# Second groups' B and C tiles moved ahead of x tiles 6 to 9, one more gate tile among the scan's chunks, two PSUM edits in the turn

## The chip, the cores and the metric

One core of a Trainium2 chip runs the whole program. The metric is the device time of one execution in microseconds (us), the median of several runs. The engines named here are PE (TensorE, matmuls), DVE (VectorE), ACT (ScalarE), POOL (GpSimd) and SP (SyncE, which only issues transfers here). Each works through its own queue in order.

## The reference

One layer of a hybrid decoder step over 1024 prompt positions and 8 sample positions (1032 columns), width 1024. Cut to what matters:

```
hn = rmsnorm(x, norm1_w);  proj = hn @ w_in
z, xbc, dt_raw, v = split(proj, [1536, 1536 + 2048, 1536 + 2048 + 24])
xbc = silu(causal_dwconv(xbc, conv_buf, conv_w, conv_b))        # width 4
xs, bm, cm = split(xbc)                                         # 24 heads x 64 | 4 groups x 64 | 4 groups x 64
dt = softplus(dt_raw + dt_bias);  a = -exp(a_log)
# chunked scan, chunks of 128 positions
cb = einsum('bclgn,bcsgn->bclsg', cc, bc)
mix = cb * decay * dt;  y_diag = einsum('bclsgr,bcsgrp->bclgrp', mix, xc)
chunk_states = einsum(bc, decay_to_end * dt, xc);  h = chunk_decay * h + chunk_states
y_off = einsum(cc, h_in, exp(acum))
y = (y_diag + y_off + d_skip * xs) * silu(z);  y = grouped rmsnorm(y)
x = x + concat([y, pool_mixer(v)]) @ w_out
u = causal_dwconv(rmsnorm(x) @ w_up);  x = x + (silu(gate) * val) @ w_down
```

The states after the step are outputs too.

## The kernel before

Everything is held transposed: a tile has 128 channels on the partitions and the 1032 positions along the free axis. The input projection has 32 such tiles, each eight k-tiles deep: x tiles 0 to 11, B tiles 12 and 13, C tiles 14 and 15 (the conv tiles, which get conv and SiLU), z tiles 16 to 27 (the gate tiles) and four pooling tiles. Tiles 12 and 14 are B and C of the first two state groups (q = 0, heads of x tiles 0 to 5), tiles 13 and 15 those of the second two (q = 1, x tiles 6 to 11).

A float32 weight is split into a high and a low part (ACT copies the high part, `lo_eng`, DVE or POOL, subtracts the low one), so a product costs three matmuls. `gemm` takes a tile in three chunks of 344 columns: 24 matmuls into one of the PSUM banks of tag g (three in this part of the program), then ACT copies the result out. In front of each chunk `gemm` runs the work due from `later` and then calls `between`, if there is one.

A conv tile (`conv_tile`) loads its weights by two transfers on SP, sets the borders of its buffer u with two small POOL operations, copies the three chunks into u on ACT (L464 to L467), copies the new conv state on POOL, then multiplies by the first tap on ACT (L477), adds three taps on DVE (L479), and in front of the next chunk asks ACT for the SiLU. A gate tile (`gate_tile`) copies z out on ACT (L652), and in front of a later chunk takes its SiLU and multiplies it into the x tile on DVE (L657, L659); after each third tile the group norm follows (squares on ACT, sums on POOL, L679 on PE, L688 on DVE).

The scan runs over eight chunks of 128 positions for each q. One step of it is made of three parts:

- `decay(q, c)`: a broadcast transfer into `mix`, a clamp on DVE (L501), twelve exponentials on ACT, and for c > 0 the same for `ce`, with a product on POOL (L516).
- `turn(q, c)`: PE transposes B of the chunk (L528) into a bank of tag pM, of which there is one, and ACT copies it to bT. PE forms C·B (L534) and transposes three x tiles (L537) into each of two banks of tag pT; DVE copies the x part to `xd` (L538), masks the C·B part (L539), scales xd (L541) and multiplies the mask product into `mix` (L546).
- `apply(q, c)`: PE forms the chunk's state into pM (L560) and its output into two banks of tag pY (L583, L593); POOL decays the old state (L569), DVE adds the new one (L573, which frees pM), and DVE adds the output to the x tiles (L601).

`ssd_tasks(q)` puts ten tasks into a queue: the first decay, and steps c = -1 to 7, each of which applies chunk c, turns chunk c + 1 and starts the decay of chunk c + 2. `between` adds a rate to a credit in front of every projection chunk and takes one task for each full credit. The rate is 0.6, starting from 0.35, for the scan's tasks: three tasks in five chunks. The sample positions have a task for each x tile (`sample_tile`): a state load, five POOL operations, a store, a reduction on DVE (L638) and an update of the x tile (L639), all with single buffers.

The order in `ssd_phase` before is: conv tiles 1 to 5; tiles 6 to 11 with the scan's tasks of q = 0; tiles 13 and 15 with six samples at rate 1.0; gate tiles 0 to 5 with the scan's tasks of q = 1, which bring the other six samples along. Behind that, in `project`, with other PSUM pools, come gate tiles 6 to 11, the pooling groups, the output projection and then the FFN. The order of the source is not the order of execution: when the program is built, each engine's list is ordered by a simulated timeline (`schedule_with_timeline_sim=True`), with the dependencies and the number of buffers kept.

Of the kernel before, what the change touches and what calls it, by code (L numbers as in the profile page):

```python
# [12 lines left out]
AF = mybir.ActivationFunctionType  # L13
# [59 lines left out]
class Kernel:  # L73
# [445 lines left out]
    def turn(self, q, c, mix):  # L519

        nc = self.nc
        cols = slice(c * P, (c + 1) * P)
        b, cc = self.bt[q], self.ctl[q]
        xd = self.ph.tile([P, 2, 12, 64], F32, tag="xd", name=self.nm("xd"), bufs=1)
        cb = self.ph.tile([P, 2, P], F32, tag="cb", name=self.nm("cb"), bufs=1)
        bT = self.ph.tile([P, P], F32, tag="bT", name=self.nm("bT"), bufs=1)
        pc = self.bank("pM")
        nc.tensor.transpose(pc[:, 0:P], b[:, cols], self.ident)  # L528
        nc.scalar.activation(bT, pc[:, 0:P], AF.Copy)

        pts = [self.bank("pT") for _ in range(2)]
        for g, pt in enumerate(pts):
            rows = slice(64 * g, 64 * g + 64)
            nc.tensor.matmul(pt[:, 384:512], b[rows, cols], cc[rows, cols], start=True, stop=True)  # L534
        for g, pt in enumerate(pts):
            for i in range(3):
                nc.tensor.transpose(pt[:, i * P : (i + 1) * P], self.xs[6 * q + 3 * g + i][:, cols], self.ident)  # L537
            nc.vector.tensor_copy(xd[:, 0, 6 * g : 6 * g + 6].rearrange("p r x -> p (r x)"), pt[:, :384])  # L538
            nc.vector.tensor_tensor(out=cb[:, g], in0=pt[:, 384:512], in1=self.mat[:, M_TRI : M_TRI + P], op=ALU.mult)  # L539
        hs = slice(c * NH + 12 * q, c * NH + 12 * q + 12)  # L540
        nc.vector.tensor_tensor(  # L541
            out=xd[:, 1], in0=xd[:, 0], in1=self.wd[:, hs].unsqueeze(2).broadcast_to([P, 12, 64]), op=ALU.mult
        )
        for g in range(2):
            part = mix[:, 6 * g : 6 * g + 6]
            nc.vector.tensor_tensor(  # L546
                out=part, in0=part, in1=cb[:, g].unsqueeze(1).broadcast_to([P, 6, P]), op=ALU.mult
            )
        return xd, bT
# [142 lines left out]
    def project(self):  # L692

        nc, d, tc = self.nc, self.d, self.tc
        self.bcd = self.dram.tile([2, NB, 2 * P], F32, name="bcd")
        self.xs, self.bt, self.ctl = [None] * XT, {}, {}

        with ExitStack() as outer:
            with self.banks(g=3, pT=2, pY=2, pM=1) as self.ps:
                self.startup([(n, n) for n in (12, 14, 0)])  # L700
                self.pu = outer.enter_context(tc.tile_pool(name="u", bufs=1))
                with tc.tile_pool(name="ssd", bufs=1) as self.ph:
                    self.ssd_phase()
            with self.banks(g=4, pT=2, pY=1, pM=1) as self.ps, tc.tile_pool(name="mix", bufs=1) as self.ph:
                for i in range(6, 12):
                    self.gate_tile(16 + i, i, None)
                self.pool_groups()

    def ssd_phase(self):
        nc, d = self.nc, self.d  # L710
        self.hst = {}
        queue = []

        credit = [0.0, 0.0]

        def between():
            credit[0] += credit[1]
            while credit[0] >= 1.0 and queue:
                credit[0] -= 1.0
                queue.pop(0)()  # L720
            if not queue:
                credit[0] = 0.0

        def flush():
            while queue:
                queue.pop(0)()

        def ssd_tasks(q):
            dec, trn = {}, {}

            def start():
                dec[0] = self.decay(q, 0)

            def step(c):
                if c >= 0:
                    self.apply(q, c, *dec.pop(c), *trn.pop(c))
                if c + 1 < NCH:
                    trn[c + 1] = self.turn(q, c + 1, dec[c + 1][0])
                if c + 2 < NCH:
                    dec[c + 2] = self.decay(q, c + 2)  # L740
                if c == -1:
                    self.sample_bc(q)
                if q == 1 and 1 <= c < 7:
                    sample(5 + c)

            queue.append(start)
            for c in range(-1, NCH):
                queue.append(lambda c=c: step(c))

        def sample(i):  # L750
            with self.behind(self.pl):
                self.sample_tile(i // 6, i)

        self.lo_eng = nc.gpsimd
        for n in range(1, 6):
            self.keep(n, self.conv_tile(n, n, None))
        ssd_tasks(0)
        credit[:] = 0.35, 0.6
        for n in range(6, 12):
            self.keep(n, self.conv_tile(n, n, between))  # L760
        flush()
        self.lo_eng = nc.vector
        for i in range(6):
            queue.append(lambda i=i: sample(i))
        credit[1] = 1.0
        for n in (13, 15):
            self.keep(n, self.conv_tile(n, n, between))
        flush()
        nc.sync.dma_start(d["conv_o"], self.conv_st)
        ssd_tasks(1)  # L770
        credit[:] = 0.35, 0.6
        for i in range(6):
            self.gate_tile(16 + i, i, between)
        flush()
        self.run_due()
# [697 lines left out]
```

## Time and profile before

| | us |
|---|---|
| median of 3 runs | 1450.8 (1449.79 to 1450.92) |
| the profiled execution | 1453.59 |
| its span in the profile | 1451.8 |
| PE busy in the span | 1376.6 (95%) |
| DVE busy | 976.9 (67%) |
| ACT busy | 701.4 (48%) |
| POOL busy | 517.4 (36%) |

The span is what the profiler's records cover; the difference to the execution's time lies around it. A busy time is a sum over stages with different limits, so it is read stage by stage. Rows of a timeline give the start, the duration, engine, line, operation, output and inputs, and in brackets the idle time of that engine just before and what ended it. "Granted clock" is the share of TensorE's full clock; it is 1.00 or 0.50 at any moment here, and a mean between in a longer stretch.

### The profile page before, as it was taken

How to read it: one execution, taken by the hardware profiler on the slowest of the kernel's cores; microseconds unless marked ns; L12 is line 12 of the kernel's file. 1: busy time of each engine (PE TensorE's matmuls, PEld its weight loads, DVE VectorE, ACT ScalarE, POOL GpSimd, SP SyncE). 2: the span in 40 equal slices, each digit the busy share in tenths (PEclk: the TensorE clock that was granted, in tenths of full speed). 3: DMA queues.
4: the chain of work that ended last, by engine and by line, in shares of the span. 5: the costliest groups of instructions: out<-in, count | busy, mean ns of one | idle time of the engine just before them, and what ended most of it. 6: DMA issues, size and time to landing. Idle time of an engine off the chain costs nothing.

```text
span 1451.8 us, 26584 instructions
## 1 busy us (share of the span) xinstructions
PE 1376.6 (95%) x10312; PEld 1325.7 (91%) x10312; DVE 976.9 (67%) x1474; ACT 701.4 (48%) x1396; POOL 517.4 (36%) x581
## 2 busy tenths in 40 slices
PE   8999999788899999999969999999999998999997
PEld 6899879768699999999959999999999998999997
DVE  6475998587853484744786777777777775567743
ACT  6247763465455451312454455554555554444441
POOL 5242566567421105765342222212222213113121
PEclk9999999999899999999989999999999999999999
DMA  6031334244311146676467778777777769457513
GB/s 241 8 105 52 117 128 149 91 139 120 109 39 39 45 144 234 229 239 195 141 152 159 204 190 201 187 204 185 189 177 194 201 217 346 135 187 234 176 51 118
DMA packets 126683, 227.56 MB, mean 157 GB/s; under 512 B 27852, under 2 KB 45084, under 8 KB 126556
## 3 DMA queue, kind: packets, MB, share of 16 engines
q1 hardware_dynamic: 88620, 143.62, 31.9%
q0 software_dynamic: 24208, 61.30, 17.2%
q10 hardware_dynamic: 13728, 20.93, 4.5%
q8 instruction: 81, 1.33, 0.4%
q14 instruction: 46, 0.38, 0.1%
HBM read 169.11 MB, written 45.15 MB: 148 GB/s over the span
## 4 chain that ended last, share of the span: by engine, by line
PE 81%; DVE 10%; DMA 3%; issue 3%; ACT 1%; POOL 1%; SPq 0%; DVEq 0%; ACTq 0%; POOLq 0%
PE g L1025 30%; PE g L1172 16%; PE g L157 10%; PE g L156 10%; PE g L158 10%; DMA mix<-acd 1%; DVE mix L546 1%; DVE mix L501 1%; PE pY L583 1%; DVE xs L601 1%; DVE xs L479 1%; DVE x L932 1%; DVE op L208 1%; DVE wop L138 1%; DVE xd L541 1%
## 5 line engine op out<-in xcount | busy, mean ns | idle before, releaser
L1025 PE MATMUL g<-op,wop 128*128 128x258 f32 x3696 | 451.3, 285 | 15.8 <-ACT wop L137 5.8
L1025 PEld LDWEIGHTS g<-op,wop 128*128 128x128 f32 x3696 | 449.8, 191 | 17.1 <-ACT wop L137 6.0
L1172 PE MATMUL g<-op,wop 128*128 128x258 f32 x1848 | 231.1, 288 | 9.2 <-ACT op L207 5.6
L1172 PEld LDWEIGHTS g<-op,wop 128*128 128x128 f32 x1848 | 228.0, 193 | 11.2 <-ACT op L207 6.0
L137 ACT ACTIVATE wop<-raw 128x512 fp32r<-128x512 f32 (+1 forms) x208 | 125.8, 607 | 229.8 <-PE g L158 126.7
L156 PE MATMUL g<-hh,wop 128*128 128x344 f32 x696 | 227.3, 327 | 4.2 <-ACT u L464 3.5
L158 PE MATMUL g<-hh,wop 128*128 128x344 f32 x696 | 226.6, 326 | 0.0
L157 PE MATMUL g<-hl,wop 128*128 128x344 f32 x696 | 225.8, 324 | 0.0
L138 DVE TENSOR_TENSOR wop<-raw,wop 128x512 fp32r<-128x512 f32 (+1 forms) x186 | 139.4, 756 | 119.0 <-ACT wop L137 113.4
L137 ACT ACTIVATE wop<-s 128x512 fp32r<-128x512 f32 (+1 forms) x136 | 83.5, 619 | 134.7 <-PE g L1172 47.3
L1004 POOL DMA_DIRECT2D s<-s x44 | 38.3, 870 | 284.9 <-DMA s<-wup 123.8
L156 PEld LDWEIGHTS g<-hh,wop 128*128 128x128 f32 x696 | 132.9, 191 | 7.2 <-ACT u L464 4.1
L158 PEld LDWEIGHTS g<-hh,wop 128*128 128x128 f32 x696 | 132.7, 191 | 1.3 <-issue 1.1
L157 PEld LDWEIGHTS g<-hl,wop 128*128 128x128 f32 x696 | 133.0, 191 | 0.6 <-issue 0.5
L1072 DVE SCALAR_TENSOR_TENSOR acc<-u,cst,acc 128x1048 f32<-128x1048 f32 x88 | 115.1, 1308 | 11.6 <-ACT acc L1070 10.1
L138 DVE TENSOR_TENSOR wop<-s,wop 128x512 fp32r<-128x512 f32 (+1 forms) x136 | 91.2, 677 | 34.8 <-ACT wop L137 32.4
L1060 DVE TENSOR_TENSOR u<-u,g 128x258 f32<-128x258 f32 (+2 forms) x176 | 58.6, 356 | 83.3 <-PE g L1025 81.0
L1057 ACT ACTIVATE u<-g 128x258 f32<-128x258 f32 (+2 forms) x220 | 69.5, 340 | 81.9 <-PE g L1025 76.3
L157 PE MATMUL g<-yl,wop 128*128 128x344 f32 x288 | 92.6, 323 | 3.0 <-DVE yl L208 3.0
L1142 POOL DMA_DIRECT2D g<-td x77 | 41.9, 548 | 143.9 <-DVE op L208 69.0
L158 PE MATMUL g<-yh,wop 128*128 128x344 f32 x288 | 92.4, 322 | 0.0
L156 PE MATMUL g<-yh,wop 128*128 128x344 f32 x288 | 91.9, 322 | 0.0
(265 smaller groups left out, 2294.6 us busy)
## 6 DMA issues: line engine op xcount, KB each, us to landing
s<-wup SPq DMA_DIRECT2D x88, 256.0 KB, 3.2
g<-td POOLq DMA_DIRECT2D x77, 258.0 KB, 4.5
raw<-wup SPq DMA_DIRECT2D x66, 256.0 KB, 4.4
raw<-win SPq DMA_DIRECT2D x58, 256.0 KB, 2.6
mix<-acd SPq DMA_DIRECT2D x16, 768.0 KB, 6.0
td<-acc ACTq DMA_DIRECT2D x22, 516.0 KB, 5.7
s<-wup POOLq DMA_DIRECT2D x44, 256.0 KB, 5.5
s<-s POOLq DMA_DIRECT2D x44, 256.0 KB, 3.9
```

What stands on the lines that cost most here:

```text
L137: self.nc.scalar.activation(hi, raw[:, :w], AF.Copy)
L138: lo_eng.tensor_tensor(out=lo, in0=raw[:, :w], in1=hi.bitcast(F32), op=ALU.subtract)
L156: nc.tensor.matmul(ps[:, :n], wh, xh[:, sl], start=(first and k == 0), stop=False)
L157: nc.tensor.matmul(ps[:, :n], wh, xl[:, sl], start=False, stop=False)
L158: nc.tensor.matmul(ps[:, :n], wl, xh[:, sl], start=False, stop=(final and k == last))
L1004: nc.gpsimd.dma_start(t, raw[acc] if acc in raw else w[acc][j], accum_op=ALU.add)
L1025: nc.tensor.matmul(out, a, b, start=(p in OPENS and j == 1), stop=(j == 12), skip_group_check=True)
L1057: a = nc.scalar.activation(out, ps[:, s], AF.Copy, scale=-1.0 if p in ("p5", "p4") else 1.0)
L1060: nc.vector.tensor_tensor(out=out, in0=out, in1=ps[:, s], op=op)
L1072: nc.vector.scalar_tensor_tensor(out=acc, in0=u[:, k : k + FW], scalar=self.c("fw", 3 * n + k), in1=acc, op0=ALU.mult, op1=ALU.add)
L1142: self.loaded = self.nc.gpsimd.dma_start(st[:, j], self.td[i + j][ROW[p]]).ins
L1172: self.pe = nc.tensor.matmul(out, a, b, start=(s == 0 and i == 0 and j == 0), stop=(s == len(PIECES) - 1 and i == nk - 1 and j == 2),).ins
```

## The change

The transposed B goes into a bank of tag g; the copy of the transposed x goes from DVE to ACT; conv tiles 13 and 15 come ahead of tiles 6 to 9 among the first groups' tasks; tiles 10 and 11 come with the samples, at rate 0.7 and without emptying the queue behind them; gate tile 0 follows at that rate, ahead of the second groups' tasks' own rate, which now runs over gate tiles 1 to 6; gate tile 6 leaves the part behind.

```diff
@@ turn
-        pc = self.bank("pM")
+        pc = self.gps()
         nc.tensor.transpose(pc[:, 0:P], b[:, cols], self.ident)
...
-            nc.vector.tensor_copy(xd[:, 0, 6 * g : 6 * g + 6].rearrange("p r x -> p (r x)"), pt[:, :384])
+            nc.scalar.activation(xd[:, 0, 6 * g : 6 * g + 6].rearrange("p r x -> p (r x)"), pt[:, :384], AF.Copy)
@@ project
-                for i in range(6, 12):
+                for i in range(7, 12):
                     self.gate_tile(16 + i, i, None)
@@ ssd_phase
         ssd_tasks(0)
         credit[:] = 0.35, 0.6
-        for n in range(6, 12):
+        for n in (13, 15, 6, 7, 8, 9):
             self.keep(n, self.conv_tile(n, n, between))
         flush()
         self.lo_eng = nc.vector
         for i in range(6):
             queue.append(lambda i=i: sample(i))
-        credit[1] = 1.0
-        for n in (13, 15):
+        credit[1] = 0.7
+        for n in (10, 11):
             self.keep(n, self.conv_tile(n, n, between))
-        flush()
         nc.sync.dma_start(d["conv_o"], self.conv_st)
+
         ssd_tasks(1)
+        self.gate_tile(16, 0, between)
         credit[:] = 0.35, 0.6
-        for i in range(6):
+        for i in range(1, 7):
             self.gate_tile(16 + i, i, between)
         flush()
         self.run_due()
```

## The prediction

> **What bounds the kernel now.** I read the slices of the page first, then the busy time by stage, then PE's waits, then the timelines of PE, ACT and DVE at the place of the longest wait. The PE row of the page says that TensorE is the engine to look at, and that the eighth to the eleventh of its 40 slices (36.3 us each), in the chunked scan, hold the longest run in which it isn't full:
>
> ```profile
> PE   8999999788899999999969999999999998999997
> ```
>
> The view by stretches (columns: stretch, length, then busy us of PE, PEld, DVE, ACT, POOL with their instruction counts, the granted clock, DMA share, GB/s):
>
> ```profile
> 139.00:240.00 101.00, 95.50 (x838) 83.67 (x837) 93.60 (x135) 68.98 (x156) 60.72 (x47) 1.00 0.40 127
> 240.00:283.50 43.50, 34.29 (x216) 33.42 (x215) 26.48 (x26) 11.81 (x21) 26.66 (x26) 0.99 0.38 118
> 283.50:411.00 127.50, 114.46 (x847) 96.75 (x848) 106.80 (x157) 74.19 (x164) 76.68 (x47) 0.90 0.35 107
> 280.00:290.00 10.00, 6.55 (x28) 6.33 (x29) 6.42 (x10) 7.65 (x21) 0.00 (x0) 0.66 0.17 55
> ...
> 411.00:483.00 72.00, 72.00 (x446) 70.08 (x445) 24.02 (x36) 37.04 (x54) 10.03 (x6) 1.00 0.13 41
> ```
>
> Call the first three stages A (x tiles with the first groups' chunks), B (B and C tiles with the samples) and C (gate tiles with the second groups' chunks). PE idles 101.00 - 95.50 = 5.5 us in A, 9.2 in B and 13.0 in C. In C the granted clock is 0.90, so another 127.5 x 0.10 = 12.8 us go to half-speed stretches. Together 40.5 us, the most that the change can win. The last row is the stretch behind them, gate tiles alone: PE 72.00 of 72.00 at clock 1.00. So what PE gains ahead of 411 us is kept there; and 18 projection chunks in 72 us make 4.0 us a chunk. In C DVE is busy 106.80 of 127.50 (84%), in A 93.60 of 101.00 (93%): the scan is near DVE's limit, and PE's gaps are its echo.
>
> PE's waits in 60 to 430 us (waiter, whom it waits for, total us, times, longest):
>
> ```profile
> PE pM L528 <- DVE h L573: 9.4, 6, 3.4
> PE pT L534 <- ACT xs L185: 5.7, 1, 5.7
> PE pY L583 <- DVE mix L546: 4.2, 3, 2.2
> PE g L156 <- ACT u L464: 3.5, 2, 2.5
> ```
>
> Three of these four are what the edits aim at: the transposed B waiting for bank pM, the second groups' first chunk waiting for a SiLU, and the mask product.
>
> **Part 1, the order of the tiles.** The 5.7 us are one wait. PE's row, then ACT's and DVE's around it:
>
> ```profile
> 283.45 0.80 PE L534 MATMUL pT<-xs,xs 64*128 64x128 f32 x4 [5.71 <-ACT xs L185]
> ```
>
> ```profile
> 271.89 0.46 ACT L652 ACTIVATE z<-g 128x344 f32<-128x344 f32 x1
> 282.32 1.08 ACT L185 ACTIVATE xs<-xs 128x1056 f32<-128x1056 f32 x1 [9.96 <-DVE xs L479]
> ...
> 288.24 0.43 ACT L652 ACTIVATE z<-g 128x344 f32<-128x344 f32 x1
> ```
>
> ```profile
> 273.43 1.30 DVE L479 SCALAR_TENSOR_TENSOR xs<-u,cst,xs 128x1056 f32<-128x1056 f32 x1
> 279.01 0.69 DVE L638 TENSOR_REDUCE dx<-stt 128x8 f32<-128x512 f32 x1 [4.27 <-POOL stt L637]
> 279.61 1.31 DVE L479 SCALAR_TENSOR_TENSOR xs<-u,cst,xs 128x1056 f32<-128x1056 f32 x1
> ```
>
> The SiLU of the last C tile sat 9.96 us at the head of ACT's queue, because DVE's three conv taps (L479) were cut in two by a sample's reduction (L638) that waited 4.27 us for POOL. PE stood from 277.74 to 283.45, and the clock of 280 to 290 us was 0.66: 3.4 us more. Gross 9.1 us.
>
> By the credits, before, the second groups' first turn is asked for ahead of the third chunk of gate tile 0: two chunks (8 us) behind the last conv tile. After, B and C are ready since the first two tiles, the last conv tile is x tile 11, and three chunks of gate tile 0 and two of gate tile 1 (20 us) come first. The 12 us more exceed the 5.7. The samples spread too: at 0.7 a chunk, four fall into x tiles 10 and 11 and two into gate tile 0, against three in each of tiles 13 and 15. What is late next: PE may run two chunks on, but the z of gate tile 0's second chunk was copied only at 288.24, behind the SiLU in ACT's queue. If that SiLU is as late as now, the copy ends near 283.45 + 0.4 and PE, out of its three g banks one chunk past 277.7 (281.7), waits about 2 us. If the fifth and sixth sample stand behind the taps it waits nothing. I take the middle, 1.1: **-8.0 us** (bounds -9.1 and 0).
>
> The moved tiles issue what they issued: each two weight loads on SP, two small POOL fills of u, one conv_st copy. The low weight parts of tiles 13 and 15 go from DVE to POOL, and those of 10 and 11 from POOL to DVE: no change in sum. The conv_o store still waits on SP for the last conv tile's copy on POOL, with the gate weights behind it, as now. The two L464 waits (3.5 us) in B come from the same queue of SiLU and samples; I leave them (bounds -3.5 and, with six samples at the same POOL pace, +3.5). Gate tile 6 moved ahead of the boundary costs PE the same three chunks; it fills scan gaps rather than a stretch that is 72.00 of 72.00 busy. Without gaps to fill it is worth nothing.
>
> **Part 2, copies from DVE to ACT.** Groups of the view by form (busy us, mean ns, idle before): DVE in C (283 to 411 us), then ACT in C, then DVE in A (108 to 241 us).
>
> ```profile
> L546 DVE TENSOR_TENSOR mix<-mix,cb 128x768 f32<-128x768 f32 x16 | 23.1, 1442 | 0.1
> ...
> L538 DVE COPY xd<-pT 128x384 f32<-128x384 f32 x16 | 8.8, 547 | 3.6 <-PE pT L537 2.8 <-PE pY L583 0.7
> L539 DVE TENSOR_TENSOR cb<-pT,mat 128x128 f32<-128x128 f32 x16 | 4.4, 278 | 0.0
> ```
>
> ```profile
> L185 ACT ACTIVATE mix<-mix,acl 128x128 f32<-128x128 f32 x96 | 28.9, 388 | 19.0 <-DVE mix L501 19.0
> ...
> L566 ACT ACTIVATE h<-pM 128x384 f32<-128x384 f32 x1 | 0.5, 493 | 0.0
> ```
>
> ```profile
> L546 DVE TENSOR_TENSOR mix<-mix,cb 128x768 f32<-128x768 f32 x16 | 17.3, 1082 | 0.8 <-ACT mix L185 0.8
> ```
>
> Sixteen copies of 547 ns leave DVE in C: 8.8 us, and A issues the same sixteen. ACT takes each at the 493 ns of L566, the same shape out of a bank: 7.9 us a stage, on top of 68.98 in 101.00 and 74.19 in 127.50, so ACT comes to 76% in A and 64% in C. In C DVE is the limit for 84% of the time: 0.84 x 8.8 = 7.4, less a little for the copies' hand-over, **-7 us** (bounds 0 and -8.8). Not more, because the product L546 is 1442 ns here against 1082 in A with POOL beside it, and that doesn't go. In A the loss is only 5.5; I take **-4** together with part 3 (bounds 0 and -5.5).
>
> **Part 3, the bank of the transposed B.** Two rows of the view by stretches, of the places behind the two longest of its waits:
>
> ```profile
> 320.00:330.00 10.00, 6.62 (x57) 5.88 (x56) 10.00 (x12) 6.17 (x17) 7.56 (x6) 0.84 0.49 172
> 340.00:350.00 10.00, 9.56 (x53) 9.11 (x54) 7.35 (x17) 7.50 (x16) 3.14 (x3) 0.83 0.92 232
> ```
>
> The 9.4 us of L528 go, since a g bank was emptied two chunks earlier. In A (2.4 of them) that is gain. In C (7.0) the h add that PE waited for was late because DVE's line was full; PE now passes it, runs on into projection matmuls, and meets L583 waiting for L546 of the same line. So I count nothing beyond part 2 (bounds 0 and -7.0, and -3.3 of clock, 10 us at 0.84 and 10 at 0.83).
>
> The price: three g banks now carry sixteen more tenants. A bT copy stuck behind a SiLU in ACT's queue would hold one; cover is the chunk that PE has in the other banks, 4.0 us; without it each 2 us more of SiLU wait are 2 us of PE.
>
> **Sum:** -8 - 4 - 7 = -19 us against the profiled execution, 1453.59 us (span 1451.8 and 1.8 around it): 1434.6. The median shown is 2.8 below that execution, so about 1432.
>
> **Rivals.** (1) *The stall moves.* The order on each engine comes from a timeline simulated at build, not from the source: the first turn stood in the source ahead of gate tile 0's third chunk and ran inside gate tile 1's first. If it is again put where SiLU 11 is late, part 1 gives nothing: -11, 1440. Against it: the source distance grows by 12 us.
> (2) *Two readers of one bank.* The copy on ACT and the cb product on DVE (L539) read one pT bank. If one has to wait for the other, two products of 278 ns and their hand-over lie in the chain of each of 16 steps: 16 x 0.56 = 9 us given back: -10, 1441. No row shows ACT and DVE in one pT bank. The Trainium skill, PSUM — Partial Sum Buffer, section PSUM bank collisions raise a hardware error, says that two engines may not be in one bank and quadrant at once, two reads included; by that rule the build must order them, and no run here shows it yet.
> (3) *ACT's queue, slower than before.* ACT waits 19.0 us in C at the heads of the exponentials for L501, 2.4 a step. A copy queued behind that wait holds xd, thus L541, L560 and the bank. With that wait before the copy in every step of both stages (16 x 2.4 = 38 us), a third covered by PE's chunks, 25 us come on and only part 1's 8 and part 2's 11 go off: +6, 1457. It decides from 1.2 us of uncovered delay a step (19/16). For it: ACT runs in order and DVE's copy never stood behind exponentials. Against it: the copies of a turn come ahead of the next-but-one chunk's exponentials in the source.
> (4) *More.* With DVE relieved the gaps in C fall under what costs the clock, and half of C's 25.8 us goes: -5 - 9 - 13 = -27, 1424.
>
> **Chances.** Forecast 0.45, (1) 0.18, (2) 0.10, (3) 0.14, (4) 0.13. A measurement of this kernel can tell about 0.2% (2.9 us) from no change. Faster: 0.45 + 0.13 and 0.22 of the 0.28 of (1) and (2), 0.80; the other 0.06 within; slower 0.14. The range, 1418 to 1452, leaves out (3) and what may lie beyond (4).
>
> **What would show it.** Right: no wait of L528; no L534 wait on the SiLU and a clock of 1.00 at the end of B; sixteen L538 copies of about 0.49 us on ACT in each stage and DVE's busy time in C near 98; PE's waits in C on L546 shorter in sum than 11 us. Wrong: waits of PE on z or u copies (L652, L464) of over 4 us, L541 waiting on ACT's L538, or half clock at the boundary of B and C as now.

## The result, and the profile after

The changed kernel takes **1460.9 us** (median of 5 runs, 1457.3 to 1462.5) against 1450.8 before: ratio 1.0066, 95% interval 1.0045 to 1.0087. It is slower by about 10 us, where 1432 was forecast, and lies 9 us above the range. The profiled execution of after took 1460.94 us (span 1459.2), 7.4 us more than that of before.

The same view by stretches as in the prediction, of the kernel after (length, busy us of PE, PEld, DVE, ACT, POOL, granted clock, DMA share, GB/s). The last row takes the scan as a whole:

```profile
139.00:240.00 101.00, 95.02 (x754) 80.50 (x753) 75.76 (x108) 73.22 (x167) 49.35 (x41) 0.93 0.33 104
240.00:283.50 43.50, 41.09 (x291) 39.96 (x290) 33.45 (x36) 13.24 (x24) 32.79 (x30) 1.00 0.47 145
283.50:411.00 127.50, 109.37 (x785) 91.29 (x784) 95.60 (x131) 80.33 (x179) 71.70 (x50) 0.89 0.35 111
...
127.00:430.00 303.00, 276.48 (x2050) 240.83 (x2050) 219.29 (x296) 184.31 (x399) 158.92 (x125) 0.93 0.34 106
```

And the last row's like of before:

```profile
127.00:430.00 303.00, 275.26 (x2089) 243.79 (x2088) 239.83 (x334) 174.46 (x370) 168.99 (x127) 0.95 0.35 109
```

DVE was relieved of 20 us, just as the change says, and PE's busy time is no lower. What grew is the time at half clock: before lost 27.7 us of idle PE and 303 x 0.05 = 15.2 of clock, together 43; after lost 26.5 and 303 x 0.07 = 21.2, together 48. (The clock is given to two places, so each sum is good to some 1.5 us.) Over the whole spans the granted clock is 0.968 against 0.973, or 46.7 against 39.2 us, and these 7.5 us are about what the two executions differ by. PE's waits of after, 60 to 440 us, show that the idle time has other causes than before:

```profile
PE pT L534 <- DVE cb L539: 16.6, 5, 6.3
PE g L156 <- ACT z L652: 5.2, 2, 2.6
PE g L156 <- ACT u L464: 2.4, 2, 1.6
PE pY L583 <- DVE mix L546: 1.3, 1, 1.3
```

The waits of L528 (9.4) and of L534 on the SiLU (5.7) are gone, and those of L583 on L546 fell from 4.2 to 1.3. In their place L534 waits 16.6 us, in five places, for the mask product that empties its pT bank. Three of the five, from PE's timelines:

```profile
159.54 0.44 PE L537 MATMUL pT<-mat,xs 128*128 128x128 f32 x2
161.23 0.27 PE L528 MATMUL g<-mat,xs 128*128 128x128 f32 x1
161.43 1.53 PE L583 MATMUL pY<-mix,xd 128*64 128x128 f32 x24
...
171.24 0.79 PE L534 MATMUL pT<-xs,xs 64*128 64x128 f32 x2 [3.48 <-DVE cb L539]
...
220.50 0.48 PE L534 MATMUL pT<-xs,xs 64*128 64x128 f32 x2 [2.50 <-DVE cb L539]
...
400.15 0.79 PE L534 MATMUL pT<-xs,xs 64*128 64x128 f32 x2 [6.29 <-DVE cb L539]
```

The rows of after by stretches that hold the first two:

```profile
220.00:230.00 10.00, 9.51 (x49) 7.11 (x51) 4.49 (x8) 7.74 (x19) 1.83 (x1) 0.66 0.00 0
170.00:180.00 10.00, 8.76 (x48) 7.78 (x50) 4.40 (x7) 9.32 (x22) 3.25 (x2) 0.66 0.00 0
```

Each of them has a clock of 0.66: 6.8 us at half speed, up to 3.4 us of work lost at gaps of 3.48 and 2.50 us. Stage A, where before had a clock of 1.00, now has 0.93. DVE isn't full: it is busy for 4.4 of these 10 us, and for 75.76 of 101.00 in stage A, against 93.60 before. ACT's timeline ahead of the first gap, and DVE's at it:

```profile
162.32 1.08 ACT L185 ACTIVATE xs<-xs 128x1056 f32<-128x1056 f32 x1 [2.39 <-DVE xs L479]
163.41 1.28 ACT L178 ACT_TABLE_LOAD   x1
164.70 3.62 ACT L185 ACTIVATE mix<-mix,acl 128x128 f32<-128x128 f32 x12
168.23 0.83 ACT L185 ACTIVATE ce<-ce 128x768 f32<-128x768 f32 x1
169.08 1.28 ACT L178 ACT_TABLE_LOAD   x1
170.37 0.87 ACT L538 ACTIVATE xd<-pT 128x384 f32<-128x384 f32 x2
```

```profile
170.90 0.29 DVE L539 TENSOR_TENSOR cb<-pT,mat 128x128 f32<-128x128 f32 x1 [0.66 <-ACT xd L538]
```

Read it backwards. PE had the transposes of this turn done at 159.98. Their copy could not have run before 162.96 on any engine, since `xd` has one buffer, which the matmuls of the chunk before (L583) read until then. It stood in ACT's queue behind a SiLU that waited for the conv taps, a table load, twelve exponentials, `ce` and another table load, and ran at 170.37, 7.4 us later. The mask product on DVE followed it, and only then was the bank free for the C·B of the next turn. The bracket names DVE's L539, because it came last; the delay is ACT's.

The second gap is of another kind. ACT's row and DVE's rows ahead of it, and then those ahead of the wait of 2.47 us that ends at 369.59:

```profile
217.38 0.87 ACT L538 ACTIVATE xd<-pT 128x384 f32<-128x384 f32 x2
...
217.87 2.37 DVE L501 SCALAR_TENSOR_TENSOR mix<-acl,mix 128x1536 f32<-128x1536 f32 x1
220.16 0.47 DVE L539 TENSOR_TENSOR cb<-pT,mat 128x128 f32<-128x128 f32 x2
```

```profile
364.29 0.87 ACT L538 ACTIVATE xd<-pT 128x384 f32<-128x384 f32 x2
...
368.11 1.23 DVE L659 TENSOR_TENSOR xs<-xs,z 128x8 f32<-128x8 f32 x1
369.26 0.28 DVE L539 TENSOR_TENSOR cb<-pT,mat 128x128 f32<-128x128 f32 x1
```

Here ACT's copies were over 1.9 and 4.1 us before the product began, and DVE had other work in front of it: a clamp of the next decay, or the group norm, the output adds and the gate products. The wait of 1.91 us that ends at 336.06 is like them, with 5.0 us between copy and product. So 6.9 of the 16.6 us are made by the product's place in DVE's line. Before, DVE took a turn's first product right behind its copy; with the copy on ACT, other work stands between. At 400 us ACT is late again, with a z SiLU in place of the conv tile's, and the product then waits another 0.8 us for the gate product on DVE.

### The profile page after: what moved, and what is told of

Its sections match the earlier page's. It is cut to its first block, busy times and chain, and to the rows that moved or that the text cites. A ratio compares the mean times of both kernels' runs of the same rounds, so it can differ in the third digit from the quotient of the medians.

```text
span 1459.2 us, 26569 instructions
## 1 busy us (share of the span) xinstructions
PE 1383.0 (95%) x10312; PEld 1328.2 (91%) x10312; DVE 958.0 (66%) x1442; ACT 713.1 (49%) x1428; POOL 496.9 (34%) x581
## 4 chain that ended last, share of the span: by engine, by line
PE 80%; DVE 7%; ACT 4%; DMA 3%; POOL 2%; issue 2%; SPq 0%; DVEq 0%; ACTq 0%; POOLq 0%
PE g L1026 30%; PE g L1173 15%; PE g L156 10%; PE g L157 10%; PE g L158 10%; ACT mix L185 1%; PE pY L583 1%; DMA st<-st_ssm 1%; DVE mix L546 1%; PE pY L593 1%; POOL st L635 1%; DVE mix L501 1%; DVE op L208 1%; DVE x L933 1%; ACT L178 1%
## 5 line engine op out<-in xcount | busy, mean ns | idle before, releaser
L1173 PEld LDWEIGHTS g<-op,wop 128*128 128x128 f32 x1848 | 227.6, 193 | 12.4 <-ACT op L207 6.1
L138 DVE TENSOR_TENSOR wop<-raw,wop 128x512 fp32r<-128x512 f32 (+1 forms) x186 | 133.9, 726 | 116.8 <-ACT wop L137 116.0
```

What stands on the lines that cost most here:

```text
L138: lo_eng.tensor_tensor(out=lo, in0=raw[:, :w], in1=hi.bitcast(F32), op=ALU.subtract)
L1173: self.pe = nc.tensor.matmul(out, a, b, start=(s == 0 and i == 0 and j == 0), stop=(s == len(PIECES) - 1 and i == nk - 1 and j == 2),).ins
```

## The experiments

The three edits are called R (the order of the tiles), P (the transposed B in a g bank, L528) and X (the xd copies L538 on ACT); after is R, P and X together. Ratios are against before, with runs of before on the same chip beside them. The letters in the expectations name theories, which the text behind them takes up.

### One edit at a time

Each kernel is before with one part of the diff above, or (e_rp) after with X undone:

```diff
@@ e_rp, turn
-            nc.scalar.activation(xd[:, 0, 6 * g : 6 * g + 6].rearrange("p r x -> p (r x)"), pt[:, :384], AF.Copy)
+            nc.vector.tensor_copy(xd[:, 0, 6 * g : 6 * g + 6].rearrange("p r x -> p (r x)"), pt[:, :384])
```

> The change with the copy of the transposed x back on DVE (L538 as before), all else as changed. Theory Q (the copies in ACT's queue hold the pT banks, because the mask product L539 waits for the copy and the next C.B matmul waits for both): the 16.6 us of L534 waits and the half-speed stretches behind them go, 1435 to 1445 us, faster than before. Theory O (the new order of tiles is what costs): it stays at 1455 or above. Theory G (the transposed B takes a g bank from the projection): it stays at 1455 or above, with waits of the projection on L652 or L464.

> The kernel before with the copy of the transposed x on ACT and nothing else. Theory Q: slower than before by 5 to 20 us, with new waits of PE at L534 for the mask product L539. Theories O and G: faster than before by 3 to 10 us, since 17.6 us leave DVE and neither the order nor the bank is changed.

> The new order of tiles alone: transposed B in pM and the copies on DVE as before. Theory Q: faster than before by 5 to 10 us, the 5.7 us wait of L534 on the SiLU gone and the L528 waits still there. Theory O: slower than before by 5 us or more.

> The transposed B in a g bank alone, order and copies as before. Theory Q: no L528 wait; DVE's line stays as full, so 0 to 6 us faster. Theory G: slower than before by 3 us or more, with more waits of the projection on the copies out of g banks.

| | ratio | 95% interval | median us |
|---|---|---|---|
| e_r | 0.9982 | 0.9966 to 0.9998 | 1447.3 |
| e_x | 0.9959 | 0.9942 to 0.9977 | 1443.0 |
| e_p | 0.9995 | 0.9981 to 1.0009 | 1448.2 |
| e_rp | 0.9988 | 0.9973 to 1.0004 | 1447.7 |

No edit is slower by itself. R is worth 2.6 us, X 5.9, and P nothing that can be measured; their sum is -9.3 us, and together they cost +9.6. Every theory that puts the loss down to one edit is out: Q, which had e_x slower by 5 to 20 us and e_rp at 1435 to 1445, O, which had e_r slower, and G, which had e_p slower. The 19 us come from the edits' being together.

### Two edits, and the first cures

e_px and e_rx are pairs. e_bt2 gives the changed kernel a second bT buffer, and e_cbfirst puts the mask product ahead of the copy in the source:

```diff
@@ e_bt2, turn
-        bT = self.ph.tile([P, P], F32, tag="bT", name=self.nm("bT"), bufs=1)
+        bT = self.ph.tile([P, P], F32, tag="bT", name=self.nm("bT"), bufs=2)
@@ e_cbfirst, turn
+            nc.vector.tensor_tensor(out=cb[:, g], in0=pt[:, 384:512], in1=self.mat[:, M_TRI : M_TRI + P], op=ALU.mult)
             nc.scalar.activation(xd[:, 0, 6 * g : 6 * g + 6].rearrange("p r x -> p (r x)"), pt[:, :384], AF.Copy)
-            nc.vector.tensor_tensor(out=cb[:, g], in0=pt[:, 384:512], in1=self.mat[:, M_TRI : M_TRI + P], op=ALU.mult)
```

> Transposed B in a g bank and the copies on ACT together, in the order of tiles before. Theory B (the g bank lets the transpose of B run early, its copy to the single bT buffer then stands in ACT's queue waiting for L560 of the chunk before, and the copies of x stand behind it): the gain of the copies on ACT alone (6 to 8 us) is gone, 1450 to 1460 us, with L529 waiting for L560 10 us or more. Theory I (new order and copies on ACT disturb each other): the two gains add, about 1441 us, as the bank alone was worth about nothing.

> New order of tiles and copies on ACT, transposed B in pM as before. Theory B: the two gains roughly add, 1437 to 1443 us, faster than before. Theory I: 1452 or above, as the whole change.

> The whole change with two buffers for bT instead of one. Theory B: L529 no longer waits for L560, and most of the loss goes: 1438 to 1450 us. Theory I, and theory K (two readers of a pT bank, L539 behind L538, are what costs): it stays at 1455 or above, with the L534 waits on L539 as in the whole change.

> The whole change with the mask product L539 ahead of the copy L538 in the source, so that DVE no longer waits for ACT's copy of the same bank. Theory K: the L534 waits shrink and DVE runs freer: 1450 or below. Theory B: the bank is still held until ACT's copy has run, behind bT's: unchanged within noise, 1456 to 1463 us, with L534 waiting for L538 instead.

| | ratio | 95% interval | median us |
|---|---|---|---|
| e_px | 1.0096 | 1.0068 to 1.0125 | 1461.1 |
| e_rx | 0.9991 | 0.9973 to 1.0010 | 1447.4 |
| e_bt2 | 1.0049 | 1.0031 to 1.0067 | 1455.9 |
| e_cbfirst | 0.9967 | 0.9948 to 0.9987 | 1444.1 |

P and X together are the loss, and in the old order of tiles it is larger still (1461, just above theory B's range and far above I's 1441). R on top of X gives up some 0.5% of their sum, and P then costs the rest; e_rx lies between the ranges of B and I.

Theory B, the single bT buffer, had a row for it. ACT's waits of after, then of e_bt2, in 127 to 430 us:

```profile
ACT bT L529 <- PE pM L560: 13.7, 5, 7.1
```

```profile
ACT bT L529 <- PE g L528: 0.2, 1, 0.2
```

In after the copy of bT stood at the head of ACT's queue for 13.7 us until the matmuls of the chunk before (L560) had read the old bT. The second buffer removes that wait, L534 waits 19.2 us for the product, and the time stays within the error of after's. It is a wait off the path, and B is out.

Theory K, two readers of one bank, is borne out in its premise. Where ACT's copy is first the product waits for it; in e_cbfirst the copy waits for the product. To turn the two around takes 1.0% off the changed kernel. PE's waits of e_cbfirst, 60 to 440 us:

```profile
PE g L156 <- ACT bT L529: 5.5, 2, 4.3
PE pY L583 <- DVE mix L546: 4.5, 2, 3.3
PE g L156 <- ACT u L464: 3.2, 2, 1.9
PE g L156 <- ACT z L652: 2.9, 2, 1.9
```

No L534 wait is left. ACT's queue now shows in the g banks, but these are three banks and not two, and the time is lower.

### Is it the bank's link with the copies, or the early place of L534?

e_late holds L534 back until the last L583 of the chunk before; e_px_cbf and e_x_cbf have the product first, without the new order of tiles.

```diff
@@ e_late, turn
-            nc.tensor.matmul(pt[:, 384:512], b[rows, cols], cc[rows, cols], start=True, stop=True)
+            with self.behind(self.applied):
+                nc.tensor.matmul(pt[:, 384:512], b[rows, cols], cc[rows, cols], start=True, stop=True)
```

> The whole change, with each turn's C.B matmuls (L534) put behind the last mask-product matmul (L583) of the chunk before in PE's order. Theory E (with its own bank free, the next turn is placed ahead of the state and output matmuls of the present chunk; PE, in order, then stands at L534 for the copies in ACT's queue with that work behind it): 1437 to 1450 us, L534 waits under 4 us in all. Theory K (the mask product chained behind ACT's copy costs wherever the turn stands): 1453 us or above, with L534 still waiting for L539.

> Bank and copies in the order of tiles before, with the mask product ahead of the copy in the source. Theories K and E: the 1.0 percent loss of bank and copies together becomes a gain, 1437 to 1446 us. If the gain of product first came with the new order of tiles only, it stays at 1455 or above.

> Copies on ACT alone with the mask product ahead of the copy. Theory K: a little better than the copies alone, 1437 to 1443 us, as only 1 to 4 us of waits on L539 were there to win. Theory E: as the copies alone, 1440 to 1445 us.

| | ratio | 95% interval | median us |
|---|---|---|---|
| e_late | 1.0061 | 1.0037 to 1.0084 | 1458.2 |
| e_px_cbf | 1.0043 | 1.0022 to 1.0064 | 1456.3 |
| e_x_cbf | 0.9941 | 0.9916 to 0.9965 | 1442.4 |

PE's waits of e_late:

```profile
PE g L156 <- ACT z L652: 7.9, 2, 4.9
PE pY L583 <- issue: 5.2, 1, 5.2
PE g L156 <- ACT bT L528: 4.3, 2, 2.9
PE g L156 <- ACT u L464: 3.8, 3, 3.1
```

The 16.6 us of L534 are gone and the time is that of after: the wait went over into the g banks (z, bT, u; line numbers are one less there) and a stretch of 5.2 us for which the profile shows no releaser. So the row that fills most of PE's idle time in after is a place where the loss shows, not what makes it, and theory E is out; theory K has the time but not its sign, the L534 waits. Nor is the product's place the whole of it: with P and X it gives back 0.5% of 0.96%, and e_px_cbf's 1456 is outside the range of K and E. The 1442 of e_x_cbf fits both theories and decides nothing.

### Whose queue carries the copy of bT

In these kernels one line moves the copy of the transposed B from ACT to DVE; e_rx_cbf is e_rx with the product first.

```diff
@@ e_btdve, turn
-        nc.scalar.activation(bT, pc[:, 0:P], AF.Copy)
+        nc.vector.tensor_copy(bT, pc[:, 0:P])
```

> The whole change with the copy of the transposed B out of its g bank on DVE instead of ACT. Theory A (that copy, L529, stands in ACT's queue: there it waits for the state matmul L560 and for SiLUs, and it holds both a g bank and everything behind it on ACT): 1438 to 1450 us, waits of the projection and of L534 on ACT's work 12 us or less in all, against 24 in the whole change. Theory C (ACT's queue is late for the copies of x whatever is done with the transposed B): 1453 or above, with the L534 waits on L539 still over 10 us.

> The whole change without its bank part (transposed B in pM) and with the mask product ahead of the copy. Theory A: the bank part costs in this setting as it did in the order before (1.0043 with it, 0.9941 without), so it comes out below the whole change with the product first, 1436 to 1443 us. Theory C: the same as that, 1440 to 1447 us.

> Old order of tiles, transposed B in the g banks, xd copies on ACT (e_px, which took 1.0096 of before), with only the copy of the transposed B moved from ACT to DVE. Theory A (the copy of bT in ACT's queue is what makes the two edits cost together): 0.994 to 1.000 of before, the L528 waits on bT gone, half-speed time in the scan below the 44 us of e_px's trace. Theory C (ACT is late for the xd copies whatever bT does): 1.006 to 1.012, and the L534 waits on the mask product stay at 8 us or more.

> The changed kernel with both cures at once: the mask product ahead of the copy (which alone gave 0.9967) and bT's copy on DVE (which alone gave 0.9991). If the two cure one and the same loss, the ratio is no better than the better of them, 0.996 to 0.999. If they cure different losses, the gains add: 1.0066 - 0.0099 - 0.0075 = about 0.989, with 0.987 to 0.993 counted as that.

> Control for the two kernels with bT's copy on DVE: here only the copy of the transposed x is on ACT and the transposed B stays in pM (the edits that gave 0.9959), with bT's copy on DVE. Theory A (bT's copy costs only where a g bank lets it come ahead of the xd copies): no gain, 0.994 to 0.999. Rival W (moving bT's copy to DVE is worth about 0.8% wherever the xd copies are on ACT, with no link to its bank): 0.986 to 0.990.

> The same control with the new order of tiles (which gave 0.9991 with bT's copy on ACT). Theory A: 0.997 to 1.002. Rival W: 0.989 to 0.993.

| | ratio | 95% interval | median us |
|---|---|---|---|
| e_btdve | 0.9991 | 0.9973 to 1.0009 | 1446.3 |
| e_rx_cbf | 0.9947 | 0.9927 to 0.9968 | 1441.8 |
| e_px_btdve | 1.0012 | 0.9992 to 1.0032 | 1451.1 |
| e_cbf_btdve | 0.9940 | 0.9918 to 0.9961 | 1440.8 |
| e_x_btdve | 0.9990 | 0.9969 to 1.0011 | 1448.2 |
| e_rx_btdve | 0.9993 | 0.9976 to 1.0010 | 1447.7 |

Set out by what the g bank alone adds, in per cent of the time before (each a difference of two ratios, so good to about 0.3):

| the g bank (P) added to | old order of tiles | new order |
|---|---|---|
| both copies: xd on DVE, bT on ACT | -0.05 | +0.06 |
| xd on ACT, bT on ACT | +1.37 | +0.75 |
| xd on ACT, bT on DVE | +0.22 | -0.02 |
| xd on ACT behind the product, bT on ACT | +1.02 | +0.20 |

The bank costs only where ACT has the copy of bT and the copies of xd both, and with the product first it costs nothing that can be measured in the new order of tiles. The controls e_x_btdve and e_rx_btdve settle that this isn't a gain which bT's copy on DVE brings anywhere (rival W, 0.986 to 0.993): with the transposed B in pM it brings nothing, and in the old order it takes away 0.3% (0.9959 to 0.9990), which is part of why the bank's cost there falls. So theory A holds in its times, in both orders (e_px_btdve lies just above the 1.000 that it allowed; e_rx_cbf fits both theories), and C is out by its times. The two cures together (0.994) are better than e_btdve; against e_cbfirst the intervals overlap, and neither of the two outcomes named, 0.996 to 0.999 and 0.987 to 0.993, was met.

Theory A missed with its waits. PE's waits of e_btdve:

```profile
PE pT L534 <- DVE cb L539: 15.3, 4, 6.8
PE g L156 <- ACT z L652: 5.2, 2, 2.9
```

They are nearly after's, and yet the time is 0.75% less. In the two longest of the four, 4.8 and 6.8 us, ACT's copies were over 4.9 us before the product, which stood behind the gate products (L657, L659) on DVE: moving bT's copy does nothing for that. In e_px_btdve, too, L534 waits 8.7 us for the product, as C had it, and the clock is 0.93, as in e_px; what shrank is PE's idle time in the scan, 21.9 us against 26.9. The row of e_btdve by stretches says where its profiled execution got the 0.75%: idle 24.6 us against 26.5, and a clock of 0.95 against 0.93, so 40 us lost against 48:

```profile
127.00:430.00 303.00, 278.43 (x2102) 243.50 (x2101) 223.34 (x319) 184.91 (x390) 160.50 (x127) 0.95 0.34 108
```

### The same turn without the bank

e_x is the cleanest partner for the gap at 171 us, since its ACT copies are just as late. Its PE rows, then its ACT rows:

```profile
158.26 0.88 PE L537 MATMUL pT<-mat,xs 128*128 128x128 f32 x6
...
165.75 0.27 PE L528 MATMUL pM<-mat,xs 128*128 128x128 f32 x1
...
173.19 0.49 PE L534 MATMUL pT<-xs,xs 64*128 64x128 f32 x2
```

```profile
170.13 0.87 ACT L538 ACTIVATE xd<-pT 128x384 f32<-128x384 f32 x2
...
171.23 0.30 ACT L529 ACTIVATE bT<-pM 128x128 f32<-128x128 f32 x1
```

The copies come at 170.13, 11 us after the transposes, for the same reasons as in after. But here the transposed B of the next turn needs pM, and the built order puts L528 4.5 us later than in after and has PE do 57 projection matmuls between the output of the chunk before and the next L534, and only 24 in after. PE reaches L534 at 173.19, when the bank is free, and waits for nothing. In this turn, then, the order with pM held the next turn back until ACT had caught up; with the g bank it starts more than a projection chunk earlier, into a pT bank that ACT hasn't emptied. That pM is the reason for the order is the likeliest reading, but the trace shows only the order. Nor is it a rule: L534 waits for the product 1.3 us in e_x, but 8.1 in e_rx and 12.5 in e_rx_btdve, which have pM as well and are no slower than before. Over the scan, e_x loses the least of the kernels with the product behind the copy:

```profile
127.00:430.00 303.00, 283.05 (x2177) 249.42 (x2176) 228.40 (x308) 192.96 (x413) 167.67 (x128) 0.98 0.36 112
```

20.0 us idle and 303 x 0.02 = 6.1 of clock are 26, against 48 in after. (This execution lies some us below e_x's median.)

**What is shown, and what is open.** Shown by times: P and X cost together, and only with bT's copy on ACT. Shown by traces: the gaps above, step by step, some of ACT's making and some of DVE's. Open is by which waits bT's copy acts over the whole scan. It isn't its wait for its own buffer (e_bt2), and not the L534 waits alone (e_late, e_btdve). Each edit also changes the order that is built on every engine, and one profile of each kernel can't separate that from the clock, which costs more behind one gap than behind another of the same length (last section). e_rp is the exception to any sum of waits: its g banks wait on ACT more than after's, and it is no slower than before. PE's waits of e_rp:

```profile
PE g L156 <- ACT z L652: 12.0, 5, 6.7
PE g L156 <- ACT u L464: 6.3, 3, 3.3
```

**A better version.** e_x_cbf (xd copies on ACT, mask product first, nothing else) takes 0.9941 of before, e_rx_cbf 0.9947 and e_cbf_btdve 0.9940, which can't be told apart; each beats both kernels. The product first gains in each of five pairs: 0.18% in e_x, which is within the error, then 0.44 in e_rx, 0.51 in e_btdve, 0.53 in e_px and 0.99 in after.

## Why the prediction was wrong

- **What bounds the kernel** stands: the loss is in the scan's idle PE and its half-speed stretches, and a kernel that wins (e_x) wins there. That DVE's full line was the limit of C, with PE's gaps its echo, was half of it: DVE lost 20 us in the scan and PE gained no busy time.
- **Part 1**, -8: the stall went as foreseen, with no L534 wait on the SiLU and a clock of 1.00 at the boundary of B and C. Its size was off: alone it is worth 2.6 us (0.3 to 4.9), inside the bounds and far from the value taken. In e_r PE waits longer in L583 for L546, 7.1 us against 4.2 before:

```profile
PE pY L583 <- DVE mix L546: 7.1, 3, 3.6
```

- **Part 2**, -7, and -4 with part 3: the copy's price was right. ACT's group by form, after:

```profile
L538 ACT ACTIVATE xd<-pT 128x384 f32<-128x384 f32 x31 | 13.7, 488 | 9.6 <-PE pY L583 6.6 <-issue 1.8 <-PE pT L537 1.2
```

  488 ns against 493 foreseen. Alone the edit gave 5.9 us of the 11.
- **The step that failed** is that the three parts were added, with two costs put at nothing or nearly so: ACT's share of the work in parts 2 and 3, from its busy share (76% and 64%), and the hand-over from ACT's copy to DVE's product, for which part 2 took off 0.4 us (7.4 to 7). In their place the runs show 19 us of cost from the edits' being together; in the changed kernel the product put first gives back 14 us, and bT's copy on DVE 11. A busy share doesn't say how long a copy stands in the queue: at 171 us it stood 7.4 us behind a SiLU, two table loads and the exponentials, with a pT bank held. And once copy and product are on two engines, the product has its own place in DVE's line, up to 5.0 us behind the copy, with the bank still held. Part 3 did ask what a late bT copy would cost, and took one chunk in the other g banks as the cover; it priced the g banks and not the pT banks, which that same queue and then DVE's have to empty. The waits on g banks came to 7.6 us, against 4.2 before; those on pT to 16.6. And L528's wait for pM was counted only as a loss that goes: P alone gained nothing, and beside X, with bT's copy on ACT and the product behind the copy, it cost 11 to 20 us. By which waits it does so over the whole scan stays open; in the turn at 171 us, the next turn came too early for ACT.
- **Rival 2** was right in its mechanism: the two readers of a pT bank are ordered. DVE's waits of after carry it:

```profile
DVE cb L539 <- ACT xd L538: 12.4, 6, 6.6
```

  The Trainium skill (PSUM — Partial Sum Buffer, section PSUM bank collisions raise a hardware error) says that the compiler's scheduler makes two engines take turns at one bank and quadrant, two reads included; the trace agrees, with these 12.4 us. The rival's price, 9 us from the products' durations, is below the gain of putting the product first (0.99%, 14 us, in the changed kernel), and it left out that the product then inherits ACT's delay.
- **Rival 3** was the case that came: 1457 given for it, 1461 measured, with a chance of 0.14. Its place was right, the copy behind the exponentials with the bank held. Its price wasn't: it charged the heads' wait for L501, and that fell from 29.2 us in the scan (19.0 of them in C) to 12.9. Nor did it see that the queue hurts only where P is there too.
- **What would show it:** of the signs of "right", no L528 wait, no SiLU wait, L538 at 0.49 us, L546 waits under 11 us, and DVE's busy time in C near 98 (95.60 in that stretch) all came. The one on L546 could not have told, since PE's waits on it were 4.2 us before the change. Of the signs of "wrong" the z copies did, with 5.2 us. The list had no line for L534 waiting on L539, where the loss then stood, and so would have let the good signs pass for success.

## What to carry to other kernels

Before work goes to an engine with spare time, look at what stands ahead of it in that engine's queue and which buffer it will hold meanwhile; a busy share answers neither. A wait that an edit removes may be what holds a producer back until a slow consumer has emptied its bank, so edits that each relieve something should be timed together as well as alone. Where two engines read one bank, put the short reader on the critical line first.

## What the hardware showed

The clock can cost as much as the gap, and not by its length alone. In after, gaps of 3.48 and 2.50 us went with 6.8 us at half clock each (rows above), up to 3.4 us of work. In e_px a gap of 2.50 us at the same place as the second, ahead of an L534 at 220.46, cost nothing: the clock of 217 to 227 us is 1.00. A gap of 2.59 us in after cost nothing either, nor did one of 3.12 us in e_x. After's gap and the row that holds it:

```profile
290.87 0.42 PE L156 MATMUL g<-hh,wop 128*128 128x344 f32 x1 [2.59 <-ACT z L652]
```

```profile
290.00:298.00 8.00, 5.61 (x37) 4.95 (x37) 3.11 (x5) 7.97 (x20) 0.00 (x0) 1.00 0.23 76
```

The same of e_x:

```profile
351.05 0.87 PE L560 MATMUL pM<-xd,bT 128*64 128x384 f32 x4 [3.12 <-DVE xd L541]
```

```profile
350.00:358.00 8.00, 6.96 (x56) 4.49 (x56) 7.96 (x12) 4.07 (x8) 2.47 (x2) 1.00 0.30 99
```

Where two gaps followed each other the clock stayed down: in e_px a gap of 5.79 us and one of 2.78 us lie in a stretch of 15 us with a clock of 0.54:

```profile
284.00:299.00 15.00, 8.84 (x35) 8.12 (x36) 5.65 (x9) 12.71 (x33) 1.45 (x2) 0.54 0.24 67
```
